# Seven block products in place of eight in the down projection of an MLP (Trainium2, one core)

## The chip, the cores and the metric

The kernel runs as one program on one core of a Trainium2 chip. The metric is the device time of one execution in microseconds (us). Three runs of the kernel before gave 1694.85, 1695.14 and 1696.07 us, with a median of 1695.14.

## The reference

One block of an encoder over 1024 tokens of width 1024, in float32. Two branches (latent attention with 8 heads, and a bidirectional mLSTM with 4 heads) are merged by gates, and an MLP follows. The part that matters here is the end:

```
x = x + merged @ w_out
u = rmsnorm(x, norm_mlp_g) @ w_mlp_up          # (1024 x 1024) @ (1024 x 4096)
x = x + square(relu(u)) @ w_mlp_down           # (1024 x 4096) @ (4096 x 1024)
return rmsnorm(x, norm_final_g)
```

## The kernel before, in words

TensorE multiplies in the format fp32r. To keep float32 accuracy each operand is split in two: `h` is a cast to fp32r on ScalarE (line 79), and `l` is the rest, source minus `h`, by a subtraction on VectorE (line 80). A product of two blocks is then three matmuls, h by h, h by l and l by h; l by l is left out. So each operand that TensorE reads costs one instruction on ScalarE and one on VectorE, and each 128x128x512 block product costs three matmuls.

The program runs in stages. First come the input projections and the mLSTM cores (to about 390 us). Within and after them the gates are made: `gate_a` for 8 column blocks, spread among the heads, and `gate_b` for 8 more (390 to 510 us); their results go to DRAM for later. Attention follows (to 850 us), then the merge and the output projection (to 1005 us), the up projection (1036 to 1327 us) and the down projection (1327 to 1685 us).

The up projection already works with seven block products in place of eight, the Winograd form of Strassen's scheme. The 4096 hidden channels are taken as 16 pairs of 128-channel blocks (`up_pair(p)`, lines 1160 to 1187). For each pair seven products of 12 matmuls run. Their right operands, sums and differences of blocks of x ("T1" to "T4" and plain blocks), were made once and stay in SBUF. Their left operands ("S1" to "S4") are sums of weight blocks and are made on VectorE by `Pair.sums` (lines 1108 to 1123). For the first five pairs two of the seven products are done ahead of the loop. `activate` applies relu and square on ScalarE and writes the hidden block to DRAM.

The down projection is a plain product (lines 1282 to 1350). The 32 blocks of 128 hidden channels are taken in 8 groups of four (FC = 4). For each block `down_in` loads the hidden block [128, 1024] and the weight rows [128, 1024] from DRAM, and splits both. Then, for each of 8 token tiles, 24 matmuls (4 blocks, 2 halves of the columns, 3 products) run into two PSUM banks, and `finish` adds the two banks, scaled by the token's norm factor `rsq`, to the residual `xm` of that token tile (line 1321, VectorE). `xm` stays in SBUF for the whole stage (8 tiles). In the last group `finish` also makes the final norm (lines 1324 to 1329) and writes the output.

Nearly all SBUF tiles come from one pool of 46 slots of 4 KB per partition (`slot`, NSLOT = 46). Raw data that is to be split comes into a second pool of 4 buffers of the same size (`wp`, NWR = 4). PSUM has two tiles of two banks (`bankA`) and four of one (`bankB`). All loads and stores in question are issued by SyncE (SP), in order. A planner of the framework fixes the order of the instructions on each engine when the program is built: instructions have the order of the program text as their priority, and one that is not ready, or has no free slot, lets later ones pass. `tc.high_priority` moves instructions forward in this order; `finish` used it. On the chip each engine then executes its list in order.

Of the kernel before, what the change touches and what calls it, by code (L numbers as in the profile page):

```python
# [18 lines left out]
P = 128  # L19
# [19 lines left out]
def kernel(ctx: ExitStack, tc: tile.TileContext, x, positions, norm_mix_g, w_in, mla_q_norm_g,  # L39
# [748 lines left out]

    def gate_a(ms):
        for m in ms:  # L790
# [8 lines left out]
            siga.append(dt_)  # L799

    def gate_b():
        for m in range(8):
# [15 lines left out]
            dump("brb", s, lambda o, m=m: o[m])  # L818

# [268 lines left out]
    class Pair:  # L1088
# [19 lines left out]
        def sums(self):  # L1108
            a, b = self.raw
            u, v = slot([P, 2, 4, P], F32, "ws"), slot([P, 2, 4, P], F32, "ws")  # L1110
            nc.vector.tensor_tensor(out=u[:, 0], in0=b[:, 0:4], in1=b[:, 4:8], op=ALU.add)
            nc.vector.tensor_tensor(out=u[:, 1], in0=u[:, 0], in1=a[:, 0:4], op=ALU.subtract)
            h, l = slot([P, 2, 4, P], F32R, "wh"), slot([P, 2, 4, P], F32R, "wl")
            split(h, l, u)
            self.ops["S1"], self.ops["S2"] = [(h[:, i], l[:, i]) for i in range(2)]
            nc.vector.tensor_tensor(out=v[:, 0], in0=a[:, 0:4], in1=b[:, 0:4], op=ALU.subtract)
            nc.vector.tensor_tensor(out=v[:, 1], in0=a[:, 4:8], in1=u[:, 1], op=ALU.subtract)
            h, l = slot([P, 2, 4, P], F32R, "wh"), slot([P, 2, 4, P], F32R, "wl")
            split(h, l, v)
            self.ops["S3"], self.ops["S4"] = [(h[:, i], l[:, i]) for i in range(2)]  # L1120
            w = slot([P, 2, 4, P], F32R, "w22")
            split(w[:, 0], w[:, 1], b[:, 4:8])
# [6 lines left out]
    hidd = [dr.tile([P, 1024], F32, tag="hid", name=nm("hid"), bufs=DFF // P) for _ in range(DFF // P)]  # L1129
# [24 lines left out]
    def activate(p, j, r):  # L1154
# [3 lines left out]
        nc.sync.dma_start(out=hidd[2 * p + j], in_=r.rearrange("p a n -> p (a n)"))  # L1158

    def up_pair(p):  # L1160
        add = lambda o, x_, y_: nc.vector.tensor_tensor(out=o, in0=x_, in1=y_, op=ALU.add)
        r0, b1 = early.pop(p, None), None
# [7 lines left out]
        r1 = slot([P, 2, 512], F32, "r")  # L1170
# [10 lines left out]
        add(r1[:, 1], b3, u[:, 1])  # L1181
        product(b2, p, "22", "T4", False)
        add(r1[:, 0], b2, m1)
        activate(p, 1, r1)
        product(b3, p, "S4", "22", False)
        add(r0[:, 1], b3, u[:, 0])
        activate(p, 0, r0)
# [63 lines left out]
    pairs[0].sums()  # L1251
    for q in range(2):
# [18 lines left out]

    for p in range(NP):
        if p + 1 < NP:
            pairs[p + 1].load()
            if p + 1 >= EARLY:
                pairs[p + 1].plain()
            pairs[p + 1].sums()
# [97 lines left out]
```

## Time and profile before

| what | value |
|---|---|
| median of 3 runs | 1695.14 us |
| the profiled execution | 1694.64 us |
| its span, first to last instruction | 1692.9 us |
| TensorE matmul (PE) busy | 1651.5 us, 8613 matmuls |
| VectorE (DVE) busy | 927.9 us |
| ScalarE (ACT) busy | 684.2 us |
| GpSimd (POOL) busy | 188.5 us |
| moved by DMA | 139.68 MB |
| granted clock of TensorE, mean | 0.994 |

How to read it: the profile is of one execution; the 1.74 us between its time and its span lie before the first and after the last instruction. Matmuls overlap each other in the pipeline, so the sum of their durations is larger than the time that they take; the number of matmuls in a stretch tells the rate. "Idle before" is the time that an engine stood still just before an instruction, with what ended it.

### The profile page before, as it was taken

The numbers are of one execution on the slowest core, as the hardware profiler recorded it, in microseconds if no ns is written. First come the engines' busy times: TensorE is split into PE (matmuls) and PEld (weight loads), VectorE is DVE, ScalarE is ACT, GpSimd is POOL, SyncE is SP. The second block draws the span as 40 slices with busy tenths as digits, with TensorE's granted clock in tenths as the row PEclk, the third lists the DMA queues.
The fourth block names the chain that finished last, engine by engine and source line by source line (L and its number), as shares of the span: only waits on it lengthen the run. The fifth ranks groups of instructions, "written<-read, shape, count | busy, mean of one in ns | idle before, by whom it ended". The sixth has DMA issues, their size and how long they took to land. (4 is left out here: it accounts for less than half of the span.)

```text
span 1692.9 us, 21982 instructions
## 1 busy us (share of the span) xinstructions
PE 1651.5 (98%) x8613; PEld 1391.0 (82%) x8613; DVE 927.9 (55%) x1405; ACT 684.2 (40%) x1211; POOL 188.5 (11%) x363
## 2 busy tenths in 40 slices
PE   7999999999999999999999997999999999999998
PEld 6789989888879979889888875778888788888886
DVE  5776756633223287787876236654554564444424
ACT  6254444432122376666743325554444421111101
POOL 4112020100001433333300000000000000000001
PEclk9999999999999999999999998999999999999999
DMA  7111110112212000000057312543333752332002
GB/s 215 38 38 55 46 38 13 57 63 67 89 62 94 1 13 1 2 13 1 8 195 246 112 50 75 149 132 118 100 100 113 276 195 100 100 100 100 25 1 100
DMA packets 112651, 139.68 MB, mean 83 GB/s; under 512 B 5971, under 2 KB 88868, under 8 KB 112548
## 3 DMA queue, kind: packets, MB, share of 16 engines
q1 hardware_dynamic: 112516, 138.28, 25.1%
q8 instruction: 68, 1.11, 0.3%
q14 instruction: 35, 0.29, 0.1%
q10 hardware_dynamic: 32, 0.01, 0.0%
HBM read 104.71 MB, written 33.55 MB: 82 GB/s over the span
## 5 line engine op out<-in xcount | busy, mean ns | idle before, releaser
L1311 PE MATMUL b<-wh,hh 128*128 128x512 f32 x512 | 201.1, 394 | 1.1 <-DVE xm L1321 1.1
L227 PE MATMUL a<-th,wh 128*128 128x512 f32 x504 | 202.1, 401 | 0.0
L228 PE MATMUL a<-tl,wh 128*128 128x512 f32 x504 | 201.7, 400 | 0.0
L1312 PE MATMUL b<-wl,hh 128*128 128x512 f32 x512 | 201.2, 394 | 0.0
L79 ACT CAST wh<-wr 128x1024 fp32r<-128x1024 f32 (+6 forms) x118 | 111.0, 962 | 193.4 <-PE b L1312 162.6
L1321 DVE SCALAR_TENSOR_TENSOR xm<-b,rsq,xm 128x512 f32<-128x512 f32 x128 | 90.1, 746 | 157.4 <-PE b L1315 157.1
L232 PE MATMUL a<-th,wl 128*128 128x512 f32 x504 | 162.9, 400 | 0.0
L204 PE MATMUL a<-wh,th 128*128 128x256 f32 (+5 forms) x504 | 161.9, 322 | 0.2 <-ACT mo L569 0.2
L1139 PE MATMUL b<-bh,wh 128*128 128x512 f32 x384 | 152.1, 398 | 9.2 <-ACT wh L79 9.2
L205 PE MATMUL a<-wl,th 128*128 128x256 f32 (+5 forms) x504 | 160.4, 319 | 0.3 <-DVE wl L80 0.3
L206 PE MATMUL a<-wh,tl 128*128 128x256 f32 (+5 forms) x504 | 160.4, 319 | 0.0
L1315 PE MATMUL b<-wh,hl 128*128 128x512 f32 x512 | 160.1, 393 | 0.0
L1139 PE MATMUL b<-bl,wh 128*128 128x512 f32 x384 | 151.7, 395 | 0.0
L1139 PE MATMUL b<-bh,wl 128*128 128x512 f32 x384 | 150.7, 395 | 0.1
L80 DVE TENSOR_TENSOR wl<-wr,wh 128x1024 fp32r<-128x1024 f32 (+6 forms) x118 | 131.3, 1128 | 23.5 <-ACT wh L79 19.0
L306 POOL TENSOR_SCALAR m<-m 128x1 f32<-128x1 f32 (+1 forms) x40 | 9.0, 225 | 1172.7 <-ACT o L1326 830.5
L1311 PEld LDWEIGHTS b<-wh,hh 128*128 128x128 f32 x512 | 96.1, 188 | 23.7 <-DVE xm L1321 1.5
L1315 PEld LDWEIGHTS b<-wh,hl 128*128 128x128 f32 x512 | 96.1, 188 | 22.8
L1312 PEld LDWEIGHTS b<-wl,hh 128*128 128x128 f32 x512 | 96.2, 188 | 22.3
L227 PEld LDWEIGHTS a<-th,wh 128*128 128x128 f32 x504 | 94.7, 188 | 21.1 <-issue 1.0
L228 PEld LDWEIGHTS a<-tl,wh 128*128 128x128 f32 x504 | 94.7, 188 | 20.7 <-issue 0.5
L232 PEld LDWEIGHTS a<-th,wl 128*128 128x128 f32 x504 | 94.0, 188 | 21.2 <-issue 0.2
(287 smaller groups left out, 3309.8 us busy)
## 6 DMA issues: line engine op xcount, KB each, us to landing
wr<-in_w_mlp_up SPq DMA_DIRECT2D x37, 512.0 KB
hid<-r SPq DMA_DIRECT2D x32, 512.0 KB, 2.6
u<-hid SPq DMA_DIRECT2D x32, 512.0 KB, 4.5
wr<-in_w_mlp_down SPq DMA_DIRECT2D x32, 512.0 KB
wr<-in_w_in SPq DMA_DIRECT2D x24, 512.0 KB, 3.8
x<-in_x SPq DMA_DIRECT2D x8, 512.0 KB, 5.7
da<-sg SPq DMA_DIRECT2D x8, 512.0 KB, 2.6
db<-sg SPq DMA_DIRECT2D x8, 512.0 KB, 2.6
```

The source lines that it names most:

```text
L79: nc.scalar.copy(out=h, in_=src)
L80: (eng or nc.vector).tensor_tensor(out=l, in0=src, in1=h.bitcast(F32), op=ALU.subtract)
L204: nc.tensor.matmul(out=ps, lhsT=xh, rhs=wh, start=(k == 0), stop=False)
L205: nc.tensor.matmul(out=ps, lhsT=xh, rhs=wl, start=False, stop=False)
L206: nc.tensor.matmul(out=ps, lhsT=xl, rhs=wh, start=False, stop=(k == n - 1))
L227: nc.tensor.matmul(out=o, lhsT=wts[k][0], rhs=xh, start=(k == 0), stop=False)
L228: nc.tensor.matmul(out=o, lhsT=wts[k][0], rhs=xl, start=False, stop=False)
L232: nc.tensor.matmul(out=o, lhsT=wts[k][1], rhs=xh, start=False, stop=(k == n - 1))
L1139: nc.tensor.matmul(out=o, lhsT=x_[:, k], rhs=y_, start=(first and k == 0 and i == 0), stop=(k == 3 and i == 2), skip_group_check=True)
L1311: nc.tensor.matmul(out=pos[n], lhsT=a[:, ts_], rhs=wh[:, c], start=(i == 0), stop=False)
L1312: nc.tensor.matmul(out=pos[n], lhsT=a[:, ts_], rhs=wl[:, c], start=False, stop=False)
L1315: nc.tensor.matmul(out=pos[n], lhsT=b[:, ts_], rhs=wh[:, c], start=False, stop=(i == FC - 1))
```

## The change

The down projection is done in the Winograd form too. The hidden matrix is cut in two along the tokens and in two along the channels (the even and the odd block of a pair), and w_mlp_down in two along the channels and in two along its columns. Of the seven left operands three are plain blocks of the hidden matrix and four are sums or differences of blocks, and so for w_mlp_down on the right. The sums are not made in the down stage:

- The weight sums are made in the gate stages. After each of the 8 steps of `gate_a` and of `gate_b` one call of `down_sums` loads a pair of weight blocks, makes four differences on VectorE, and writes them to DRAM.
- The hidden sums are made at the end of `up_pair` by `keep`: four operations on VectorE, and seven writes of [128, 512] to DRAM in place of two of [128, 1024].
- Within `up_pair` the preparation of the next pair, which stood ahead of the call, is spread among the products, `sums` is cut in three (`sums`, `plain_22`, `sums_14`), and the raw weights are loaded a pair earlier.
- The down projection takes the 16 pairs in 4 groups of four (GD = 4). In a group, phases 0, 1 and 2 have two products each and phase 3 has one; a product covers four token tiles with 12 matmuls each. The seven partial results are added in five pairs of accumulators in SBUF ("m1", "11", "12", "22", "21"; 10 slots), and only in the last group do they come to `xm`, which is loaded at its start.

```diff
+    def down_sums(p):
+        y, z = slot([P, 2, 512], F32, "wy"), slot([P, 2, 512], F32, "wz")
...
+        nc.sync.dma_start(out=y, in_=rows[:, :, 0:512])
+        nc.sync.dma_start(out=z, in_=rows[:, :, 512:1024])
+        a, b = slot([P, 2, 512], F32, "wt"), slot([P, 2, 512], F32, "wt")
+        nc.vector.tensor_tensor(out=b[:, 1], in0=z[:, 0], in1=y[:, 0], op=ALU.subtract)
+        nc.vector.tensor_tensor(out=a[:, 0], in0=z[:, 1], in1=b[:, 1], op=ALU.subtract)
+        nc.vector.tensor_tensor(out=a[:, 1], in0=z[:, 1], in1=z[:, 0], op=ALU.subtract)
+        nc.vector.tensor_tensor(out=b[:, 0], in0=y[:, 1], in1=a[:, 0], op=ALU.subtract)
+        nc.sync.dma_start(out=wd_d[p][:, 0:2, :], in_=a)
+        nc.sync.dma_start(out=wd_d[p][:, 2:4, :], in_=b)
...
@@ gate_a, gate_b
+            down_sums(summed.pop(0))
...
+    def keep(p, r0, r1, u):
+        f = slot([P, 512], F32, "hs")
+        nc.vector.tensor_tensor(out=u[:, 1], in0=r0[:, 1], in1=r1[:, 1], op=ALU.add)
+        nc.vector.tensor_tensor(out=u[:, 0], in0=u[:, 1], in1=r0[:, 0], op=ALU.subtract)
+        nc.vector.tensor_tensor(out=r0[:, 1], in0=r0[:, 0], in1=r0[:, 1], op=ALU.subtract)
+        nc.vector.tensor_tensor(out=f, in0=r1[:, 0], in1=u[:, 0], op=ALU.subtract)
+        for j, src in ((0, r0[:, 0]), (1, r1[:, 0]), (2, u[:, 0]), (3, r0[:, 1]), (4, r1[:, 1]), (5, u[:, 1]), (6, f)):
+            nc.sync.dma_start(out=hid_d[p][:, j, :], in_=src)
...
     def up_pair(p):
+        nx = pairs[p + 1] if p + 1 < NP else None
+        if p + 2 < NP:
+            pairs[p + 2].load()
...
+        if nx and p + 1 >= EARLY:
+            nx.plain()
         product(b2, p, "S3", "T3", False)
         add(u[:, 1], b2, m1)
+        if nx:
+            nx.sums()
+        r1 = slot([P, 2, 512], F32, "r")
...
+        activate(r0)
+        keep(p, r0, r1, u)
...
+    GD = 4
+    def raw_pair(srcs):
+        r = wp.tile([P, 2, 512], F32, tag="wr", name=nm("wr"))
+        for j, src in enumerate(srcs):
+            nc.sync.dma_start(out=r[:, j], in_=src)
+        return r
+    def in_pair(srcs):
+        r = raw_pair(srcs)
+        h, l = slot([P, 2, 512], F32R, "dh"), slot([P, 2, 512], F32R, "dl")
+        split(h, l, r)
+        return [(h[:, j], l[:, j]) for j in range(2)]
...
+    def operands(p, ph):
+        if ph == 3:
+            return in_last(p)
+        right = ([down_row(p, 0)[:, 0:512], down_row(p, 1)[:, 0:512]] if ph == 0 else
+                 [wd_d[p][:, 2 * (ph - 1) + j, :] for j in range(2)])
+        return [in_pair([hid_d[p][:, 2 * ph + j, :] for j in range(2)]), in_pair(right)]
+    def take(name, pr, j, bank, fresh=False):
...
+        if fresh:
+            nc.scalar.copy(out=o, in_=bank)
+        else:
+            nc.vector.tensor_tensor(out=o, in0=bank, in1=o, op=ALU.add)
+    def dmul(o, tt, ops, j, first, order):
+        c = slice(tt * P, (tt + 1) * P)
+        for n, i in enumerate(order):
+            (ah, al), (bh, bl) = ops[i][0][j], ops[i][1][j]
...
+            nc.tensor.matmul(out=o, lhsT=ah[:, c], rhs=bh, start=st, stop=False, skip_group_check=True)
+            nc.tensor.matmul(out=o, lhsT=ah[:, c], rhs=bl, start=False, stop=False, skip_group_check=True)
+            nc.tensor.matmul(out=o, lhsT=al[:, c], rhs=bh, start=False, stop=en, skip_group_check=True)
...
+    def settle_in(name, tt, part):
+        t = tt + 4 * part[0]
+        o = acc[name, tt // 2][:, tt % 2]
+        if name != "11":
+            nc.vector.tensor_tensor(out=o, in0=o, in1=acc["m1", tt // 2][:, tt % 2], op=ALU.add)
+        c = slice(part[1] * 512, (part[1] + 1) * 512)
+        nc.vector.scalar_tensor_tensor(out=xm[t][:, c], in0=o, scalar=rsq[:, t:t + 1], in1=xm[t][:, c], ...)
+    def final(tt, part, bank):
...
+        nc.vector.scalar_tensor_tensor(out=xm[t][:, c], in0=bank, scalar=rsq[:, t:t + 1], in1=xm[t][:, c], ...)
...
+    nxt = [operands(p, 0) for p in range(GD)]
+    for g in range(NG):                     # NG = 4 groups
...
+            for tt in range(4):             # phase 0, first product (first group: operand by operand)
+                dmul(h_(tt), tt, ops, 0, True, every)
+        for pr in range(2):
+            take("m1", pr, None, b3(A[pr]), first_group)
+        nxt = [operands(p, 1) for p in group]
+        for tt in range(4):                 # second product, added in the same banks
+            dmul(h_(tt), tt, ops, 1, False, every)
...
+        nxt = [operands(p, 2) for p in group]          # between the two products of phase 1
...
+        ops, ops3 = nxt, [operands(p, 3) for p in group]
...
+        else:                               # last group, phases 2 and 3
+            for tt in range(4):
+                for name, part in (("22", (1, 1)), ("21", (1, 0)), ("12", (0, 1))):
+                    settle_in(name, tt, part)
+            for tt in range(4):
+                dmul(h_(tt), tt, ops, 1, True, every)
+                final(tt, (1, 1), h_(tt))
+                dmul(Bk[tt], tt, ops, 0, False, every)
+                final(tt, (1, 0), Bk[tt])
+                finish(tt + 4)
+                dmul(h_(tt), tt, ops3, 0, False, every)
+                final(tt, (0, 1), h_(tt))
+                finish(tt)
```

## Rows read from the trace of the kernel before

**Rows 1.** Head of the page: span, then busy time, share and instructions.

```profile
span 1692.9 us, 21982 instructions
PE 1651.5 (98%) x8613; PEld 1391.0 (82%) x8613; DVE 927.9 (55%) x1405; ACT 684.2 (40%) x1211; POOL 188.5 (11%) x363
```

**Rows 2.** What TensorE waited for, whole span: us in total, times, longest.

```profile
PE b L1139 <- ACT wh L79: 9.2, 2, 8.8
...
PE b L1311 <- DVE xm L1321: 1.1, 1, 1.1
```

**Rows 3.** Stretches of the span: busy time of each engine, granted clock, DMA.

```profile
core 0: us, PE busy (x) PEld busy (x) DVE busy (x) ACT busy (x) POOL busy (x), PEclk, DMA share, GB/s
1047.00:1117.00 70.00, 69.16 (x294) 54.45 (x295) 45.16 (x61) 30.75 (x33) 0.00 (x0) 1.00 0.46 136
1117.00:1325.00 208.00, 208.00 (x898) 167.73 (x897) 101.33 (x134) 93.04 (x109) 0.00 (x0) 1.00 0.33 107
1350.00:1440.00 90.00, 90.00 (x391) 73.04 (x390) 49.20 (x56) 22.02 (x22) 0.00 (x0) 1.00 0.47 159
1327.00:1685.00 358.00, 356.57 (x1539) 288.47 (x1537) 169.22 (x196) 72.31 (x77) 5.20 (x14) 1.00 0.32 112
80.00:400.00 320.00, 319.08 (x1911) 276.56 (x1910) 202.22 (x353) 144.64 (x333) 40.66 (x74) 1.00 0.16 46
390.00:512.00 122.00, 120.31 (x518) 97.53 (x517) 32.45 (x45) 20.55 (x25) 0.52 (x16) 0.99 0.26 83
```

**Rows 4.** Groups by line, the matmuls of the down stage: busy us, mean ns | idle before.

```profile
L1311 PE MATMUL b<-wh,hh 128*128 128x512 f32 x512 | 201.1, 394 | 1.1 <-DVE xm L1321 1.1
...
L1312 PE MATMUL b<-wl,hh 128*128 128x512 f32 x512 | 201.2, 394 | 0.0
...
L1315 PE MATMUL b<-wh,hl 128*128 128x512 f32 x512 | 160.1, 393 | 0.0
```

**Rows 5.** Groups by line and shape from 1170 us on, VectorE and ScalarE.

```profile
L1321 DVE SCALAR_TENSOR_TENSOR xm<-b,rsq,xm 128x512 f32<-128x512 f32 x128 | 90.1, 746 | 157.4 <-PE b L1315 157.1 <-DMA xm<-xmd 0.3
...
L80 DVE TENSOR_TENSOR wl<-wr,wh 128x1024 fp32r<-128x1024 f32 x38 | 46.4, 1221 | 8.3 <-ACT wh L79 8.2
L79 ACT CAST wh<-wr 128x1024 fp32r<-128x1024 f32 x38 | 39.9, 1051 | 186.6 <-PE b L1312 162.6 <-DMA wr<-in_w_mlp_down 17.9 <-DVE xm L1321 6.1
...
L1328 DVE SCALAR_TENSOR_TENSOR o<-xm,m,gf 128x1024 f32<-128x1024 f32 x8 | 10.3, 1284 | 17.8 <-POOL m L308 17.8
...
L1161 DVE TENSOR_TENSOR r<-b,r 128x512 f32<-128x512 f32 x8 | 5.5, 691 | 4.3 <-PE b L1139 4.3
...
L1112 DVE TENSOR_TENSOR ws<-ws,wr 128x512 f32<-128x512 f32 x7 | 4.8, 682 | 0.0
```

**Rows 6.** The end of the span in order of time: start us, us.

```profile
1684.03 0.62 PE L1315 MATMUL b<-wh,hl 128*128 128x512 f32 x2
1684.46 1.41 DVE L1321 SCALAR_TENSOR_TENSOR xm<-b,rsq,xm 128x512 f32<-128x512 f32 x2 [0.66 <-PE b L1315]
1685.96 1.06 ACT L1326 ACTIVATE o<-xm 128x1024 f32<-128x1024 f32 x1 [4.39 <-DVE xm L1321]
...
1688.06 1.28 DVE L1328 SCALAR_TENSOR_TENSOR o<-xm,m,gf 128x1024 f32<-128x1024 f32 x1 [2.19 <-POOL m L308]
```

**Rows 7.** What ScalarE waited for from 1340 us on.

```profile
ACT wh L79 <- PE b L1312: 162.6, 6, 32.1
...
ACT hh L79 <- DMA u<-hid: 18.8, 17, 2.8
```

**Rows 8.** What TensorE waited for from 80 to 400 us.

```profile
PE b L761 <- issue: 0.6, 1, 0.6
...
```

**Rows 9.** What ScalarE waited for from 80 to 400 us.

```profile
...
ACT raw L593 <- DVE acc L588: 20.7, 7, 7.3
...
```

**Rows 10.** DMA issues: count, KB each, median us to landing.

```profile
u<-hid SPq DMA_DIRECT2D x32, 512.0 KB, 4.5
```

**Rows 11.** Line 798 alone: durations ns min/median/max, first and last start.

```profile
L798 SPq DMA_DIRECT2D da<-sg x8: 338/338/343, 86.6 to 369.4; - x8
```

More of the change, by code (lines that the diff above doesn't have):

```diff
@@ L1128 @@
     B = {}
-    hidd = [dr.tile([P, 1024], F32, tag="hid", name=nm("hid"), bufs=DFF // P) for _ in range(DFF // P)]
+    hid_d = [dr.tile([P, 7, 512], F32, tag="hid", name=nm("hid"), bufs=NP) for _ in range(NP)]
     xmd = [dr.tile([P, 1024], F32, tag="xmd", name=nm("xmd"), bufs=8) for _ in range(8)]
@@ L1251 @@
     pairs[0].sums()
+    pairs[0].plain_22()
+    pairs[0].sums_14()
     for q in range(2):
@@ L1269 @@
     nc.vector.reciprocal(out=rsq, in_=rsq)
+    pairs[1].load()
     for p in range(NP):
[L1273 to L1277, printed above, removed]
[L1278 to L1295 removed]
@@ L1297 @@
-    nxt = [down_in(f) for f in range(FC)]
-    for f0 in range(0, NF, FC):
-        hid, wd = [n[0] for n in nxt], [n[1] for n in nxt]
-        last = f0 + FC == NF
+        up_pair(p)
+    GD = 4
[9 more added lines that the diff above has]
+        return [(h[:, j], l[:, j]) for j in range(2)]
@@ new lines, in final @@
+    def final(tt, part, bank):
+        t = tt + 4 * part[0]
+        c = slice(part[1] * 512, (part[1] + 1) * 512)
+        nc.vector.scalar_tensor_tensor(out=xm[t][:, c], in0=bank, scalar=rsq[:, t:t + 1], in1=xm[t][:, c],
+                                       op0=ALU.mult, op1=ALU.add)
+    NG = NP // GD
+    nxt = [operands(p, 0) for p in range(GD)]
+    xm = [None] * 8
+    every = range(GD)
+    for g in range(NG):
+        first_group, last = g == 0, g == NG - 1
+        group = range(g * GD, (g + 1) * GD)
@@ L1331 @@
-        nxt = []
-        for t2 in range(4):
-            pair = [(t, [bankB(), bankB()]) for t in (2 * t2, 2 * t2 + 1)]
-            if f0 == 0:
-                for t, _ in pair:
-                    xm[t] = slot([P, 1024], F32, "xm")
-                    nc.sync.dma_start(out=xm[t], in_=xmd[t])
-            if f0 == 0 and t2 == 0:
-                for i in range(FC):
-                    for t, pos in pair:
-                        down(t, i, pos)
-                for t, pos in pair:
-                    finish(t, pos)
-            else:
-                for t, pos in pair:
-                    for i in range(FC):
-                        down(t, i, pos)
-                    finish(t, pos)
-            if not last:
-                nxt.append(down_in(f0 + FC + t2))
+        ops = nxt
@@ new lines @@
+        nxt = [operands(p, 1) for p in group]
+        for tt in range(4):
+            dmul(h_(tt), tt, ops, 1, False, every)
+        for pr in range(2):
+            if last:
+                for j in range(2):
+                    settle_in("11", 2 * pr + j, (0, 0))
+                    final(2 * pr + j, (0, 0), h_(2 * pr + j))
+            else:
+                take("11", pr, None, b3(A[pr]), first_group)
+        ops = nxt
+        Bk = [bankB() for _ in range(4)]
+        for tt in range(4):
+            dmul(Bk[tt], tt, ops, 0, True, every)
+            take("12", tt // 2, tt % 2, Bk[tt], first_group)
```

120 lines of the change are left out of this document (72 added, 48 removed).

## Prediction

> **What bounds the kernel now.** I read the head of the page first: TensorE's matmuls are busy for 98% of the span, VectorE for 55%, ScalarE for 40% [rows 1]. Since matmuls overlap, the share alone proves little, so the waits of TensorE come next: the largest is one of 8.8 us ahead of the up projection, and the only one of the down stage is 1.1 us at its start [rows 2]. Then the stretches: in the down stage, 1327 to 1685 us, 1539 matmuls fill 358 us while VectorE is busy for 169 and ScalarE for 72 [rows 3]. The kernel is bound by the number of matmuls that TensorE issues, nearly everywhere. So a change gains what it takes from that number, as long as the new operands arrive in time, and work on other engines is free as long as it stays beside matmuls. The groups by line show the down stage as three lines of 512 matmuls each, 1536 in all [rows 4].
>
> **The price of a matmul.** The mean of 394 ns in its row [rows 4] is a duration with overlap. The rate is read from a stretch without a wait: 390 issues (391 records, one shared with the border) in the 90 us from 1350 on make 0.2308 us each [rows 3]. In the up stage, whose products are issued in the order h-h, h-l, l-h that the new down stage uses, 898 matmuls in 208 us make 0.2316. So the new order costs nothing per matmul, and I take 0.2308.
> The Trainium skill ("TensorE: Matmul & The Clock Gate", section "Wait — 56ns, not 53.3ns?") gives 215.7 ns from start to start for 512 columns at full clock. By it the same count would give back 41.4 us, an estimate from that page; the row is 7% slower at a granted clock of 1.00, so the row decides.
>
> **What is removed.** A group of the new stage has three phases of two products and one of a single product, seven; a product is four token tiles by 12 matmuls, 48. Seven by 48 by four groups is 1344 matmuls in place of 1536. Gone: 192 x 0.2308 = 44.3 us. The new stage then needs 1344 x 0.2308 = 310.2 us of TensorE.
>
> **What is added, stage by stage.**
>
> *Gate stages.* 16 calls of `down_sums`, each four operations of 128x512 from SBUF to SBUF. The nearest row is the weight sum of line 1112, 682 ns [rows 5]: 2.73 us a call, 43.6 us in all, half before 390 us and half after. From 80 to 400 us VectorE is busy for 202 of 320 us, from 390 to 512 for 32 of 122 [rows 3]; with the sums that is 224 of 320 and 54 of 122. Each call also has four DMAs on SP at about 0.34 us [rows 11], 1.4 us of SP's queue; the weight loads of the next step stand behind them. The cover is TensorE's lead: its largest wait in the first stretch was 0.6 us [rows 8]. What speaks for a cost are the slots: ScalarE already waits 20.7 us there at line 593 for a `raw` tile that VectorE still reads [rows 9], and each call holds four more slots for a load (4.5 us for 512 KB by the nearest load [rows 10]), its operations, and a store. Bounds: -1 us (the little that TensorE waits could fall away with a new order) to 22 us (each of the first eight calls delays a core's chain by its 2.73 us, uncovered); the later eight stand beside an engine that idles for half of the time. I take 1.5, near the row of 0.6.
>
> *Up stage.* `keep` adds four operations per pair, 2.73 us, on VectorE; seven stores in place of two add 5 x 0.34 = 1.7 us on SP. From 1047 to 1117 us, five pairs, VectorE goes from 45 to 59 of 70 us; from 1117 to 1325, eleven pairs, from 101 to 131 of 208 [rows 3]. It stays under TensorE in both, tightest in the first (84%). Queued behind `keep` on VectorE are the additions that free a PSUM bank for the next product; a bank that comes back 2.7 us late is covered by another product, 12 x 0.2308 = 2.8 us, in another bank. The raw weights come a pair (84 x 0.2308 = 19.4 us) earlier, ahead of those stores on SP, so the stores delay nothing that is due. The cut of `sums` moves work and adds none. Bounds: -0.5 (the waits there are about that) to 5 x 2.7 = 14 us; I take 0.5.
>
> *Start of the down stage.* The operands of phase 0 need 16 slots. The last pair has no successor to prepare, and each of its products frees four slots of a right operand, so they come while it runs. The first product goes operand by operand: 12 matmuls, 2.8 us, against two splits, 2 x 1.221 = 2.4 us on VectorE [rows 5]. Before, the same passage cost 1.1 us [rows 2]. I take no difference; the bounds are -1 and the four pairs of splits uncovered, 9.8 us.
>
> *Groups 1 to 3 of the down stage.* A group has 8 + 8 + 8 + 4 = 28 splits where there were 16 per 8 blocks: 112 in place of 64 (1.221 us on VectorE, 1.051 on ScalarE [rows 5]). VectorE has 28 x 1.221 = 34.2 us of splits and 28 x 0.69 = 19.3 us of adding banks to the accumulators (the 691 ns of line 1161 [rows 5], in the first group mostly on ScalarE), 53.5 us per group against 336 x 0.2308 = 77.5 us of TensorE. Loads are 28 x 512 KB per group, 189 GB/s by this sum, against 159 GB/s at a DMA share of 0.47 now [rows 3]; SP issues 56 halves, 19 us of 77.5. The four raw buffers allow 4 x 2.77 = 11.1 us from load to release, and a load takes 4.5 [rows 10] plus 2.3 for both splits. Slots: 10 accumulators, 16 for the running phase, 16 for the next: 42 of 46. The next phase can be prepared while the present one runs, so nothing is exposed. I take 0.5 us for all three; the upper end stands with the rivals.
>
> *Last group.* Two things change. `xm` and the final gain hold 9 more slots: 10 + 9 + 16 + 16 = 51 of 46, so the last three splits of phase 1, and of phase 2, start only when the phase before ends, operand by operand. The first operands are there, so TensorE is held for about one split on either engine, 1.05 + 1.22 us at most at each of two handovers less what the first operands cover; I take 1.5 each, 3 us, between 0 and the eight splits of a phase in full, 9.8 each. And VectorE must do 20 splits (24.4), the bank additions (4 x 0.69 + 8 x 0.69 = 8.3), four products straight to `xm` from the accumulator and four from the bank (8 x 0.746 = 6.0), twelve settlements (12 x (0.682 + 0.746) = 17.1), twelve last additions (9.0) and eight final products of 1.284 us (10.3): 75.1 us beside 77.5. It just fits if the settlements of "21" and "12" are moved forward into its gaps, and a backlog at the end is likely.
>
> *Tail.* After the last matmul two operations of line 1321 (1.41 us) become one, so -0.7 us; then ScalarE, GpSimd, VectorE and the store as before [rows 6]. `finish` of the other half's tile stands in the same queue and no longer has the priority that it had. With the backlog I take +1 us net, between -0.7 and 6.
>
> **Sum.** The profiled execution took 1694.64 us: 1692.9 of span [rows 1] and 1.74 around it. -44.3 + 1.5 + 0.5 + 0 + 0.5 + 3 + 1 = -37.8 gives 1656.8; the median of the runs is 0.5 us above that execution. I say 1656.
>
> **Rivals.**
>
> *The slots serialise the down stage* (slower). If the next phase's operands get no slots until the present one is done, each of the 15 handovers shows its eight splits, 8 x 1.221 = 9.8 us, 146 us in all, and the time is 1694.6 - 44.3 + 146 = 1796. It decides from 44.3 / 9.8 = 4.5 such handovers on. For it: in the old down stage ScalarE waits 162.6 us for slots that TensorE still reads [rows 7]. Against it: those waits reach 32 us and TensorE does not follow, and 42 of 46 fit by my count; it needs tiles released later than their last reader. With the last group's two handovers in full it is 1656.8 - 3 + 19.6 = 1673.
> Beside it the Trainium skill ("Perfetto Trace Analysis", section "Optimization Strategy") says that the same gap repeating on the engine that should be saturated can mean too little SBUF or PSUM for the next tile. No such gap is in this trace before; after, gaps of TensorE at the end of each phase would be this sign.
>
> *The gate stages pay for the sums.* Eight calls beside the mLSTM cores at 2.73 us, or their slots, hold the cores' chains: up to 22 us, so 1657 to 1677. For it the wait of line 593, against it 0.6 us of TensorE waiting.
>
> *The gain is nearly whole.* The planner fills all gaps: 1694.6 - 44.3 - 0.7 = 1649.6.
>
> *VectorE sets the pace in the last group.* The 75.1 us meet waits, a tenth of it is lost and the tail shows it: 8 to 10 us more than I take, 1665.
>
> That the products aren't fewer is excluded by the count.
>
> **Chances and range.** Forecast, 1652 to 1662: 0.45. Nearly whole: 0.15. Last group: 0.16. Gate stages: 0.13. Slots: 0.11, of which 0.07 ends slower. A run differs from another by some 0.1%, so 0.2% (3.4 us) is what a measurement can tell from no change. Faster 0.90; same 0.03, where slots or gate stages eat just the 44 us; slower 0.07. The range is 1648 to 1680: from just under the whole gain to just over the last group's two handovers in full, or the gate stages' upper end (1677).
>
> **What would show it.** Three groups of matmuls of 448 each at 0.231 us apart; a down stage of about 315 us; VectorE at 74% in it (112 splits 137, banks and `xm` about 92 of 310 us). TensorE's waits up to 1327 us as before within 3 us. In the last group, waits of 1 to 2 us for ScalarE's or VectorE's splits at two handovers, and VectorE without a gap in its last 33 us. It is wrong if TensorE waits regularly in the first three groups (slots, or four raw buffers too few for the loads), if waits appear before 512 us, or if the up stage's 19.4 us per pair grow.

## The result: 18.4 us gained, where 39 were forecast

The changed kernel takes 1676.56 us (median of four runs, 1676.23 to 1677.49), the kernel before took 1694.99 (also four runs); the ratio is 0.9892, with a 95% interval of 0.9875 to 0.9909. It is faster by 1.1%, and the time lies in the range (1648 to 1680), but the gain is less than half of the forecast. So 44 us of matmuls went, and some 26 us came back.

### The profile after

The head of the page, to be held against [rows 1]:

```profile
span 1675.1 us, 22459 instructions
PE 1614.1 (96%) x8421; PEld 1358.4 (81%) x8421; DVE 1051.5 (63%) x1551; ACT 745.0 (44%) x1275; POOL 196.0 (12%) x363
```

8613 - 8421 = 192 matmuls fewer: the change does what it says. TensorE's share falls from 98 to 96%, which is the first sign that it now waits. What it waits for (us in total, times, longest), against [rows 2]:

```profile
PE b L204 <- ACT wh L79: 7.6, 1, 7.6
PE b L1167 <- ACT wh L79: 7.1, 1, 7.1
...
PE a L1376 <- ACT dh L79: 4.8, 1, 4.8
PE b L1167 <- DVE u L1198: 4.7, 5, 1.1
...
PE a L1377 <- DVE dl L80: 2.7, 2, 2.0
...
PE a L1376 <- DVE xm L1401: 1.4, 1, 1.4
PE b L689 <- DVE cst L693: 1.2, 1, 1.2
```

The second row is the wait of 8.8 us ahead of the up projection [rows 2], a little shorter. The others are new or have grown: one at L204, which is the start of the latent stage (1.0 us before); five at L1167 for a `u` in the up stage (one of 0.8 us before); two kinds at the start of the down stage (`dh`, `dl`); one of 1.4 us in its last group (`xm`); and one of 1.2 us that ends at 254.8 us, in a core of the mLSTM (`cst`). The stretches of the span, with the columns of [rows 3]:

```profile
core 0: us, PE busy (x) PEld busy (x) DVE busy (x) ACT busy (x) POOL busy (x), PEclk, DMA share, GB/s
503.00:519.00 16.00, 8.42 (x34) 6.69 (x33) 10.07 (x23) 5.52 (x7) 0.00 (x0) 0.79 0.34 134
1047.00:1117.00 70.00, 65.36 (x273) 50.12 (x271) 47.74 (x70) 34.59 (x40) 0.00 (x0) 1.00 0.47 158
1117.00:1325.00 208.00, 207.63 (x896) 168.34 (x897) 136.07 (x186) 95.05 (x108) 0.00 (x0) 1.00 0.44 151
1325.00:1404.00 79.00, 70.64 (x289) 54.77 (x288) 39.46 (x39) 40.79 (x46) 0.00 (x0) 0.96 0.62 206
1404.00:1640.00 236.00, 236.00 (x1022) 191.50 (x1021) 167.10 (x173) 87.60 (x89) 0.00 (x0) 1.00 0.61 204
1640.00:1667.00 27.00, 24.56 (x103) 18.53 (x101) 15.11 (x17) 8.05 (x14) 5.98 (x14) 1.00 0.29 117
```

Read the first two columns together. From 1404 to 1640 us TensorE is full (236.00 of 236), at 236 / 1022 = 0.231 us per matmul: the body of the new down stage runs exactly as it was priced. So does the up stage from 1117 us on. What is not full are the passages between: 8.42 of 16 us around 511 us, 65.36 of 70 in the first up pairs, 70.64 of 79 at the start of the down stage.

To put a size on each passage, compare the start of the n-th matmul in both traces (n counted from the first; up to the down stage both kernels have the same matmuls, within an up pair partly in another order, and no record is missing). How much later it comes in the changed kernel:

| passage | shift at its end | what it adds | forecast |
|---|---|---|---|
| to 26 us, the first matmuls | +1.1 | +1.1 | none |
| to 503 us, gate stages (nearly all at 253 us, where the wait for `cst` stands) | +2.5 | +1.4 | 1.5, both rows together |
| 503 to 519 us, start of the latent stage | +9.2 | +6.7 | |
| 519 to 1036 us | +7.4 | -1.8 | none |
| 1036 to 1340 us, up stage (all of it before 1137) | +12.5 | +5.1 | 0.5 |
| first matmul of the down stage | +17.5 | +5.0 | 0 |
| to 1404 us, its first group | +23.7 | +6.3 | 0 |
| the rest of the down stage | | +2.0 | 3.5 |
| tail | | +0.7 | 1 |

In sum 26.5; 44.3 less 26.5 is the 17.8 by which the span is shorter (1692.9 to 1675.1). The first line is not the change's: in the profiles of the variants below, whose first microseconds are the same program, it lies between -0.4 and +1.1.

### Three passages, line by line

**At 510 us.** VectorE, ScalarE and TensorE, in order of time (start us, us; in brackets the idle time before and what ended it):

```profile
509.44 1.23 DVE L836 TENSOR_TENSOR sg<-a,sg 128x1024 f32<-128x1024 f32 x1 [2.96 <-PE a L232]
510.58 0.68 DVE L802 TENSOR_TENSOR wt<-wz,wt 128x512 f32<-128x512 f32 x1
...
512.38 0.48 DVE L407 TENSOR_TENSOR s<-posT,s 128x128 f32<-128x128 f32 x2
...
515.47 0.29 DVE L419 TENSOR_SCALAR s<-s 128x256 f32<-128x256 f32 x1
515.79 0.42 ACT L420 ACTIVATE rot<-s 128x256 f32<-128x256 f32 x1 [9.56 <-DVE s L419]
516.12 1.55 ACT L79 CAST wh<-wr 128x768 fp32r<-128x768 f32 x2
...
516.98 1.01 PE L204 MATMUL b<-wh,th 128*128 128x384 f32 x2 [7.58 <-ACT wh L79]
```

The page puts the 7.6 us down to the cast of a weight, but ScalarE had idled for 9.56 us ahead of it: its queue is in order, and the sine of the rotary tables (L420) stands before the casts. The sine waits for the tables (L407 to L419), and these stand on VectorE behind the last call of `down_sums`, which stands behind the last gate's multiplication, which waits for TensorE. In the kernel before, L412 to L419 ran from 503.0 to 505.3, ahead of that multiplication (there L814):

```profile
503.02 0.29 DVE L412 TENSOR_SCALAR s<-s 128x256 f32<-128x256 f32 x1
...
504.98 0.29 DVE L419 TENSOR_SCALAR s<-s 128x256 f32<-128x256 f32 x1
506.92 1.23 DVE L814 TENSOR_TENSOR sg<-a,sg 128x1024 f32<-128x1024 f32 x1 [1.65 <-PE a L232]
```

**At 1069 us.**

```profile
1066.50 0.69 DVE L1190 TENSOR_TENSOR u<-r,r 128x512 f32<-128x512 f32 x1 [2.22 <-ACT r L1185]
...
1068.43 0.68 DVE L1193 TENSOR_TENSOR hs<-r,u 128x512 f32<-128x512 f32 x1
...
1069.03 0.68 DVE L1198 TENSOR_TENSOR u<-b,r 128x512 f32<-128x512 f32 x1
...
1069.77 0.50 PE L1167 MATMUL b<-bh,wh 128*128 128x512 f32 x1 [1.13 <-DVE u L1198]
```

`keep` (L1190 to L1193) waits for ScalarE's squares, and VectorE idles for 2.22 us in front of it, with the addition that frees TensorE's bank queued behind. The same four lines come again at 1084, 1100 and 1116 us: four gaps of 1.5 us between matmuls.

**At 1340 us.**

```profile
1341.91 1.06 ACT L1185 ACTIVATE r<-r 128x1024 f32<-128x1024 f32 x1
1342.87 3.87 ACT L79 CAST dh<-wr 128x1024 fp32r<-128x1024 f32 x4
...
1343.00 0.69 DVE L1190 TENSOR_TENSOR u<-r,r 128x512 f32<-128x512 f32 x1 [2.21 <-ACT r L1185]
...
1345.54 4.62 DVE L80 TENSOR_TENSOR dl<-wr,dh 128x1024 fp32r<-128x1024 f32 x4
...
1344.90 1.09 PE L1376 MATMUL a<-dh,dh 128*128 128x512 f32 x2 [4.84 <-ACT dh L79]
1347.94 0.80 PE L1377 MATMUL a<-dl,dh 128*128 128x512 f32 x1 [1.96 <-DVE dl L80]
```

Not one operand of the down stage is cast before the last pair's squares are done at 1342.9, though two raw tiles had been loaded since 1300 us. Then the two splits come one after the other, with TensorE standing still.

### The profile page after: what moved, and what is told of

The parts are those of the page before. It is cut to its first block, busy times and chain, and to the rows that moved or that the text cites. A ratio compares the mean times of both kernels' runs of the same rounds, so it can differ in the third digit from the quotient of the medians.

```text
span 1675.1 us, 22459 instructions
## 1 busy us (share of the span) xinstructions
PE 1614.1 (96%) x8421; PEld 1358.4 (81%) x8421; DVE 1051.5 (63%) x1551; ACT 745.0 (44%) x1275; POOL 196.0 (12%) x363
## 4 chain that ended last, share of the span: by engine, by line
PE 86%; DVE 5%; ACT 3%; issue 3%; POOL 1%; DMA 1%; SPq 0%; POOLq 0%; ACTq 0%; DVEq 0%
PE b L1167 17%; PE a L232 7%; PE a L228 7%; PE a L227 7%; PE a L204 5%; PE a L205 5%; PE a L206 5%; PE b L1007 3%; PE a L1377 3%; PE a L1378 3%; PE a L1376 3%; PE b L1377 2%; PE b L1376 2%; PE b L1378 2%; PE a L986 2%
## 5 line engine op out<-in xcount | busy, mean ns | idle before, releaser
L79 ACT CAST dh<-wr 128x1024 fp32r<-128x1024 f32 x112 | 114.2, 1049 | 157.3 <-PE a L1377 49.0
L80 DVE TENSOR_TENSOR dl<-wr,dh 128x1024 fp32r<-128x1024 f32 x112 | 134.1, 1221 | 62.0 <-ACT dh L79 61.3
L1167 PE MATMUL b<-bh,wh 128*128 128x512 f32 x384 | 151.2, 399 | 11.6 <-ACT wh L79 7.1
L204 PE MATMUL a<-wh,th 128*128 128x256 f32 (+5 forms) x504 | 161.6, 321 | 0.2 <-ACT mo L569 0.2
L1167 PE MATMUL b<-bl,wh 128*128 128x512 f32 x384 | 152.2, 396 | 0.0
L1167 PE MATMUL b<-bh,wl 128*128 128x512 f32 x384 | 150.7, 396 | 0.0
L1377 PE MATMUL a<-dl,dh 128*128 128x512 f32 x256 | 101.9, 398 | 2.7 <-DVE dl L80 2.7
L80 DVE TENSOR_TENSOR wl<-wr,wh 128x1024 fp32r<-128x1024 f32 (+6 forms) x86 | 93.2, 1096 | 15.8 <-ACT wh L79 11.8
L1378 PE MATMUL a<-dh,dl 128*128 128x512 f32 x256 | 101.5, 397 | 0.0
L204 PEld LDWEIGHTS a<-wh,th 128*128 128x128 f32 x504 | 95.2, 189 | 6.7 <-ACT P L993 0.5
L205 PEld LDWEIGHTS a<-wl,th 128*128 128x128 f32 x504 | 95.2, 189 | 6.4 <-DVE wl L80 0.8
L206 PEld LDWEIGHTS a<-wh,tl 128*128 128x128 f32 x504 | 95.1, 189 | 5.4
L1167 PEld LDWEIGHTS b<-bh,wh 128*128 128x128 f32 x384 | 72.7, 189 | 31.8 <-ACT wh L79 8.5
```

Of the source, the lines that this page charges most:

```text
L79: nc.scalar.copy(out=h, in_=src)
L80: (eng or nc.vector).tensor_tensor(out=l, in0=src, in1=h.bitcast(F32), op=ALU.subtract)
L204: nc.tensor.matmul(out=ps, lhsT=xh, rhs=wh, start=(k == 0), stop=False)
L205: nc.tensor.matmul(out=ps, lhsT=xh, rhs=wl, start=False, stop=False)
L206: nc.tensor.matmul(out=ps, lhsT=xl, rhs=wh, start=False, stop=(k == n - 1))
L1167: nc.tensor.matmul(out=o, lhsT=x_[:, k], rhs=y_, start=(first and k == 0 and i == 0), stop=(k == 3 and i == 2), skip_group_check=True)
```

## The experiments

Each edit is made on the changed kernel unless said otherwise. The kernel before took 1694.1, 1695.0 and 1694.3 us on the three occasions; ratios are to that.

**1. The last call of the sums one step away.** Two calls at one earlier step of the second gate, none at the last:

```
-            down_sums(summed.pop(0))
+            for _ in range((1, 1, 1, 2, 1, 1, 1, 0)[m]):
+                down_sums(summed.pop(0))
```

> The changed kernel, but gate_b makes no weight sums after its last step; step 3 makes two pairs instead. Theory A: TensorE's wait of 8.0 us at the first latent product (at 509 us) comes from the last call of down_sums: its four operations stand on VectorE ahead of the rotary tables, the sine of these stands on ScalarE ahead of the casts of the latent weights. Then the wait falls back to about 1.4 us as in the kernel before, and the time goes from 1676.6 to about 1670 (-6.7, the step of the ledger between 503 and 520 us). Rival B: a general load of VectorE and of SP in the gate stage delays the weights; one call more at step 3 makes up for it and the time stays within 2 us.

Measured: 1671.98 us, ratio 0.9872 (0.9857 to 0.9886). The step between 503 and 519 us falls from 6.7 to 0.2: the tables now run from 505.85 to 508.10 us, ahead of the gate's multiplication (L836, 509.68). Of the 6.7 us that were expected some 4 are left (3.7 by the medians against the kernel before, 4.6 without it), since 1.2 us come up at the step with two calls and 1.3 us more in the down stage.

The row of 503 to 519, to be held against the same stretch above:

```profile
503.00:519.00 16.00, 14.04 (x62) 12.45 (x61) 9.54 (x17) 7.82 (x10) 0.00 (x0) 0.89 0.41 134
```

62 matmuls where there were 34; 28 x 0.231 are the 6.5 us by which the step fell.

**2. The tables first.** All sixteen calls stay where they are; the tables and the sine are emitted ahead of the second gate:

```
-    weave((gate_b(), 1.0))
     rotary()
+    weave((gate_b(), 1.0))
```

> The changed kernel with all 16 calls of down_sums in their places, but the rotary tables made ahead of gate_b. Theory A: the sine no longer stands behind the last sums, so the casts of the latent weights run early and the wait of 8.0 us is gone or nearly so: about 1670. Rival C: the sums on VectorE and their four DMAs delay the latent weights directly (loads queued on SP, rest halves queued on VectorE): the wait stays at 4 us or more and the time within 3 us of 1676.6.

Measured: 1674.51 us, ratio 0.9885 (0.987 to 0.99). The 7.6 us wait is gone, one of 3.3 us for a `wl` stands in its place, and the step falls from 6.7 to 1.8; about 2 us come up where the tables now stand. So the time falls by only 1 to 2 us, where 6.6 were expected, and the step is what tells: it is the order of sums and tables, from either side, and not the sums' work: 1.8 us of additions cannot hold TensorE for 6.7, but the 3.4 us of tables and the sine behind them can.

**3. The sums alone.** The kernel before, with the sixteen calls added and their results read by nothing:

```
             siga.append(dt_)
+            down_sums(summed.pop(0))
...
             dump("brb", s, lambda o, m=m: o[m])
+            down_sums(summed.pop(0))
```

> The kernel before with one addition: the sixteen calls of down_sums in the gate stages, whose results nothing reads; the up and down stages are those of before. It prices the sums alone. Theory A (the last call stands ahead of the rotary tables on VectorE, so that the latent stage starts late): the step of about 6.7 us between 504 and 519 us is there, with the 1.5 us at 253 us, and nothing else: 1694 + 8 = 1702 us (1700 to 1703.5). Rival (the steps in the gate stages come from what the new up and down stages do to the order of the whole program): 1694 to 1697.

Measured: 1702.23 us, ratio 1.0044 (1.0027 to 1.006), 7.3 us by the medians. The shift against the kernel before rises by 1.5 at 253 us and by 6.7 between 503 and 519, and does not grow after; the wait is the same to the tenth:

```profile
PE b L204 <- ACT wh L79: 7.6, 1, 7.6
```

So the gate stages' 8 us are the sums' alone, and neither the new up stage nor the down stage has a part in them.

**4. The last pair's seventh sum without a tile of its own.** `f` is written over `r1[:, 0]` once that has been stored, for the last pair alone:

```
-        f = slot([P, 512], F32, "hs")
+        f = r1[:, 0] if p == NP - 1 else slot([P, 512], F32, "hs")
```

> The changed kernel, but for the last pair the seventh hidden sum is written over a block that is already stored, so that it takes no slot of its own. Theory A (slots in order of the text): the tile of this sum is the last one ahead of the operands of the down stage, and it is given its slot only after the last activation, so all casts of the down stage wait for that. Without it the first four casts run beside the last pair's matmuls: TensorE's waits of 5.2 and 2.6 us at 1340 to 1348 us and the stretch at half clock behind them go, 8 to 11 us, about 1667. Rival B: four raw buffers; the operands of pairs 2 and 3 come late whatever the slots do: the first wait goes, 5 us, but waits behind it stay, about 1672. Rival C: ScalarE and VectorE are too busy at the end of the last pair: within 2 us of 1676.6.

Measured: 1666.89 us, ratio 0.9848 (0.983 to 0.9865). From the last up matmul to 1404 us the shift grows by 2.0 instead of 11.3. ScalarE in the passage:

```profile
1327.67 3.89 ACT L79 CAST dh<-wr 128x1024 fp32r<-128x1024 f32 x4
1336.09 1.06 ACT L1184 ACTIVATE r<-r 128x1024 f32<-128x1024 f32 x1 [4.53 <-DVE r L1203]
```

Four casts now run ahead of the last pair's squares, where in the changed kernel they came behind them. One tile of 128x512 had held up everything: tiles come out of one pool in the order of the program's text, `keep` of the last pair stands in it ahead of the down stage's operands, and its `hs` had to wait for a tile to come free. That an instruction without a free slot lets later ones pass, as the description of the planner says, did not help here: the four casts stand behind `hs` in the text, and they came 15 us later with it than without it.

**5. The last pair's `keep` behind the operands.** The other way round: `hs` stays, the whole `keep` is emitted later.

```
     nxt = [operands(p, 0) for p in range(GD)]
+    keep(*late.pop())
```

> The changed kernel with the last up pair's keep (its four VectorE operations, the tile of its seventh sum and its seven stores) emitted behind the operands of the down stage's first 64-matmul block, in place of ahead of them; everything it computes is unchanged, and its seventh sum keeps a tile of its own. Theory A (tiles are handed out in the order of the text: the seventh sum's tile waits for the last pair's neighbours and blocks the down stage's first casts): the 5.2 us wait at 1339.7 and the 2.6 us behind it go, as in the run that gave the sum no tile of its own: -9 us, 1667 to 1669. Rival (the stores of the last pair or its four VectorE operations hold up the down stage, not the tile): moving them behind the casts on VectorE helps too, but the loads of the last pair are late and no gain over -5 is left, 1671 to 1675.

Measured: 1666.47 us, ratio 0.9836 (0.9822 to 0.9849), the same as in 4 within its interval. The four casts stand at 1327.97, and TensorE's longest wait in the passage is 2.2 us; the shift grows by 3.7 there. Experiment 4 takes away the tile (and stores one block earlier), with `keep`'s four operations where they were; this one moves the tile and all the rest. Both bring the casts forward by the same 15 us, so the tile's place in the text is shown as the cause, and the rival's price for the late stores (no gain over 5) is not there.

**6. The order of products in the first five pairs.** S1 was emitted ahead of S3, to give VectorE more time for the addition.

```
+        if p < EARLY:
+            product(b3, p, "S1", "T1", True)
         product(b2, p, "S3", "T3", False)
```

> The changed kernel, but for the first five pairs the product S1 stands ahead of S3 in the text, so that it lies between S2 and S3, which share a bank. Theory A: TensorE's four waits of 1.5 us from 1068 to 1117 us arise because S3 follows S2 at once and has to wait until VectorE has read the bank; with S1 in between they go: -5.4, about 1671. Rival B: keep's 2.7 us on VectorE is the cause, and a bank comes back late whichever product stands there: less than 2 us gained.

Measured: 1677.14 us, ratio 0.9902 (0.9887 to 0.9916): no gain. The theory behind it fell: in pairs two to five, where the gaps lie, the operands of TensorE's matmuls follow each other in the same order by name in both traces, and S1's result is added without a wait for TensorE (1074.60 us in the changed kernel). So the order had already been S2, S1, S3: the planner had drawn S1 forward. Only the first pair, which has no gap, was reordered. TensorE waits for `u` in the same places, 5.6 us in all. It also says that the 12 matmuls of S1 do stand between, 2.8 us, and are too few.

**7. `keep` of the first five pairs one addition later.** It is emitted in the next pair, behind the first addition:

```
         add(u[:, 0], b2, m1)
+        if late:
+            keep(*late.pop())
...
-        keep(p, r0, r1, u)
+        if p < EARLY:
+            late.append((p, r0, r1, u))
+        else:
+            keep(p, r0, r1, u)
```

> The changed kernel with one move: for the first five up pairs the four VectorE operations and seven stores of keep are emitted one pair later, behind the next pair's first add (u[:, 0] = S2's bank + m1), so that this add stands ahead of them on VectorE. In the changed kernel's timeline the add runs at 1069.03, behind keep's four (1066.50 to 1069.03), which wait for ScalarE's squares, and TensorE's S3 product waits for it until 1069.77. Theory B (keep stands in front of the add that S3's bank waits for): the four waits of about 1.5 us at 1068, 1084, 1100 and 1116 go, the step of 5.4 us in the first five pairs falls to about 1, and the time falls by 4 to 5.5 us, to 1671 to 1672.5. Rival (the products' own order is the cause: fewer products of the next pair stand between those of one bank, whoever is first on VectorE): the waits stay, 1676 to 1677.

Measured: 1668.07 us, ratio 0.9844 (0.9829 to 0.9859), 3 us below what theory B said. TensorE waits for no `u` in the up stage any more. VectorE in the passage:

```profile
1064.08 0.69 DVE L1200 TENSOR_TENSOR u<-b,r 128x512 f32<-128x512 f32 x1 [1.61 <-PE b L1167]
1064.69 0.69 DVE L1190 TENSOR_TENSOR u<-r,r 128x512 f32<-128x512 f32 x1
...
1066.63 0.68 DVE L1193 TENSOR_TENSOR hs<-r,u 128x512 f32<-128x512 f32 x1
```

The addition comes as soon as TensorE has the bank ready, and `keep` fills the time in which VectorE had idled. The up stage's part of the shift goes from +5.1 to -2.0, so it is now 2 us shorter than in the kernel before; the other 1.2 us are the first matmuls, which differ from run to run. The Trainium skill ("Perfetto Trace Analysis", section "Optimization Strategy") reads a gap that repeats as a possible lack of SBUF or PSUM for the next tile. Here a gap repeated four times and went with no buffer added, so the queue's order was the cause.

**8. `keep` of the first five pairs on GpSimd.**

```
+        eng = nc.gpsimd if p < EARLY else nc.vector
-        nc.vector.tensor_tensor(out=u[:, 1], in0=r0[:, 1], in1=r1[:, 1], op=ALU.add)
+        eng.tensor_tensor(out=u[:, 1], in0=r0[:, 1], in1=r1[:, 1], op=ALU.add)
...
```

> The changed kernel with keep's four operations of the first five up pairs on GpSimd instead of VectorE, their place in the text unchanged. Theory B (keep occupies VectorE ahead of the add): the four waits of about 1.5 us go and the time falls by 4 to 5.5 us, to 1671 to 1672.5, as when keep is emitted later. Rival (the products' own order): the waits stay, 1676 to 1677. A third way: GpSimd's operations take about twice as long as VectorE's 0.69 us and hold the tiles longer, so that a later pair waits for a slot: the four waits go and others come, 1673 to 1677.

Measured: 1676.27 us, ratio 0.989 (0.9875 to 0.9905): no gain. The waits shrink, but others take their place, and the rows show another way than the one expected (tiles held longer). GpSimd's first two operations, and VectorE beside them:

```profile
1065.74 1.73 POOL L1191 TENSOR_TENSOR u<-r,r 128x512 f32<-128x512 f32 x1 [206.10 <-DVE u L1199]
1067.55 1.63 POOL L1192 TENSOR_TENSOR u<-u,r 128x512 f32<-128x512 f32 x1
```

```profile
1065.64 0.68 DVE L1135 TENSOR_TENSOR ws<-wr 128x512 f32<-128x512 f32 x1
1066.24 1.78 DVE L1137 TENSOR_TENSOR ws<-wr,wr 128x512 f32<-128x512 f32 x1
1067.94 1.78 DVE L1136 TENSOR_TENSOR ws<-ws,wr 128x512 f32<-128x512 f32 x1
...
1071.35 0.68 DVE L1199 TENSOR_TENSOR u<-b,r 128x512 f32<-128x512 f32 x1
```

The sums of the next pair's weights, 0.69 us each alone, take 1.78 and stretch the preparation that was meant to be relieved.

**9. The edits together.** Experiment 1 (here with the two calls at the gate's first step), 4 and 7:

> The changed kernel with three edits together: the last gate step's call of down_sums made at the second gate's first step instead (two calls there, none at the last), keep of the first five pairs emitted behind the next pair's first add, and the last pair's seventh sum written over a stored tile in place of a slot of its own. If the three losses are separate, their parts add: 1676.6 - 5.5 to 6.5 (latent start) - 4 to 5.5 (first pairs) - 9.3 (start of the down stage) = 1655.5 to 1658 us. If one loss takes the place of another (a wait that is only moved to the next product), 1660 to 1667.

Measured: 1656.92 us, ratio 0.9779 (0.9764 to 0.9793). The three losses are nearly separate: alone the edits gained 3.7, 8.8 and 8.5 us over the change, 21.0 in all, and together 19.6 (each by the medians against the kernel before of its occasion). At the last matmul of the up stage the shift against the kernel before is -0.3 where it was +12.5. The same kernel once more:

> The kernel with the three edits (two calls of the sums at the second gate's first step and none at its last, keep of the first five pairs behind the next pair's first add, the last pair's seventh sum without a tile of its own), as measured at 1656.9, in more rounds: 1656 to 1658.

Measured: 1656.55 us, ratio 0.9778 (0.9765 to 0.9791). In this profile the step with two calls cost 3.7 us, in the first one 1.4, of the same program. TensorE's wait there (for a `wl`, at 405 us) is 1.9 us against 1.1, and behind it the granted clock is 0.50 from 406.8 to 410.2 us, the level of 1.2 GHz, where in the first profile it stays at 1.00. Why the wait is longer is open, and it bounds what one profile can tell of a passage of this kind.

**10. The last pair's `keep` late as well.** As 9, with the edit of 5 in place of 4, so that neither the tile nor VectorE's four operations stand ahead of the operands.

> The three edits with another third one: the last pair's keep is emitted behind the down stage's first operands, so that it neither takes a tile nor VectorE ahead of them (with the seventh sum written over a stored tile, four VectorE operations of keep still stood from 1332.08 to 1334.88 ahead of the last split of the first block, and TensorE waited 1.1 us for it). If that wait is all: 1656.9 - 1.5 = 1655.4. If the last pair's stores, now later, hold up loads of the first group: 1657 to 1660.

Measured: 1655.31 us, ratio 0.9774 (0.9761 to 0.9787). The wait of 1.0 us for `dl` in the second profile of 9 is gone, that for `dh` (1.2 there, 1.3 here) has stayed; the difference of 1.2 us to 9 is within the intervals.

**11. The last group's priority restored.** As 10, with the bodies of `finish` and `final` put under `tc.high_priority(offset=HPM)`, as the kernel before had its `finish`.

> As the kernel with the late keep, and the eight finish and sixteen final of the last group put ahead of other ready work, as the kernel before had them (high_priority with the same offset). The wait of 1.75 us for xm at 1635.7 behind the output's scaling, and the 0.8 us of the tail, should shrink if their order on VectorE is their cause: 1 to 2 us less than the kernel without it. If the bank is simply handed over at once whatever the order, no difference (within 1 us).

Measured: 1654.68 us, ratio 0.9771 (0.9757 to 0.9785), 0.6 us less than 10, which is no difference that this measurement can tell. What TensorE waited for in it:

```profile
PE b L205 <- DVE wl L80: 2.0, 1, 2.0
...
PE a L1384 <- DVE xm L1411: 1.6, 3, 0.7
PE b L1384 <- ACT dh L79: 1.4, 1, 1.4
PE a L232 <- DVE wl L80: 1.3, 1, 1.3
```

The longest wait for `xm` went from 1.4 to 0.7 us, and small ones came. This is the fastest version that was run: 39.7 us below the kernel before, of the 44.3 that the matmuls are worth.

## Why the prediction was wrong

**What held.** The count and the price: 192 fewer at 0.231 us. The body of the down stage: groups without a wait from 1404 to 1640 us, so the slots did not serialise it (that rival asked for 4.5 handovers of 9.8 us). The splits came out as forecast in number and length:

```profile
L80 DVE TENSOR_TENSOR dl<-wr,dh 128x1024 fp32r<-128x1024 f32 x112 | 134.1, 1221 | 62.0 <-ACT dh L79 61.3
```

Tail: 1 forecast, 0.7 measured, with `finish` of the other tile ahead of the last `xm` on VectorE, as described.

**What came near by luck.** The last group and the groups before it: 3.5 forecast, 2.0 measured, but not by the handovers that were named. TensorE waits for no split in the last group. Its one wait there is for a bank:

```profile
1656.89 1.28 DVE L1385 SCALAR_TENSOR_TENSOR o<-xm,m,gf 128x1024 f32<-128x1024 f32 x1 [0.72 <-POOL m L308]
1658.09 0.74 DVE L1401 SCALAR_TENSOR_TENSOR xm<-a,rsq,xm 128x512 f32<-128x512 f32 x1
...
1658.89 0.50 PE L1376 MATMUL a<-dh,dh 128*128 128x512 f32 x1 [1.39 <-DVE xm L1401]
```

VectorE reads that bank (L1401) only behind the output's scaling (L1385), which itself waited for GpSimd. Nor was VectorE without a gap at the end: from 1636 to 1669 us it was busy for 20.1 of 33 us, and in the whole down stage for 67% of the time (215 of 322 us), where 74% was forecast.

**What failed.** Three terms failed, by 6.6, 4.6 and 11.3 us, 22.5 together; the lines without a term, the last group and the tail give 2.5 of it back.

**Gate stages, "I take 1.5, near the row of 0.6".** Measured 8, inside the stated bounds (-1 to 22), and with the sign that the prediction had named, waits before 512 us. The place was wrong as well as the size. I priced the first eight calls by the cores' chain and called the later eight safe, since "the later eight stand beside an engine that idles for half of the time". An idle engine is no cover for work that stands in front of something due: the 6.7 us are all the last call's, by what is queued behind it. The rival "the gate stages pay for the sums" gave the time that was found, 1657 to 1677, but by the wrong mechanism: of the 26.5 us only the 1.4 before 503 us can be the cores'. What puts the tables behind the sums is not settled: the tables' tiles come behind the sums' tiles in the text, and the planner may also have ranked them so. Moving either took the 7.6 us wait away, which does not tell the two apart. The 1.4 us at 253 us are the wait for `cst`, which also comes with the sums alone (experiment 3); what delays it was not tried.

**Up stage, "a bank that comes back 2.7 us late is covered by another product, 12 x 0.2308 = 2.8 us".** Measured 5.1, inside the bounds of -0.5 to 14. The step counted `keep`'s four operations as the lateness, and left out that they wait themselves: VectorE idled for 2.2 us for ScalarE's squares with the addition ready behind. The bank of S2 was ready at about 1065.7 us and its addition ran at 1069.03, 3.3 late, and with the addition's own 0.7 that is 4.0 against a cover of 2.8. I named what is queued behind the new work, not what the new work waits for. It ended after the first five pairs, where VectorE is tightest, as the step said; the other eleven cost nothing. But these five are also the pairs with two products made ahead of the loop, so that fewer products stand between S2 and S3, and no run tells the two reasons apart.

**Start of the down stage, "so they come while it runs ... I take no difference".** Measured 5.0 and 6.3, just beyond the upper bound of 9.8. With one tile out of the way (experiment 4), or with the same tile later in the text (experiment 5), the operands do come while the last pair runs, so the count of tiles was not the fault; their order was. I counted how many are needed, not who stands before them in the text. `keep` adds one tile per pair, 16 in all, and the last one stands ahead of the very first operand. Part of the second number is the clock: behind the wait the granted clock was at half, from 1345 to 1352 us, the level of 1.2 GHz, and the matmuls stood 0.43 us apart there. In experiment 4, where TensorE's waits in the passage were 1.5 and 0.5 us, it was 1.00 from 1325 to 1392.

**The sum as a whole.** With the three orders mended the time is 1654.7 to 1656.9, where 1656 was forecast. The matmuls were priced rightly; what failed is that the new work would be placed well by itself. That the mended sum meets the forecast so closely is in part luck: the mended up stage gives 2.0 us back (experiment 7), which no term had.

## What to carry on

Work that is moved beside an idle engine is priced in two numbers, not in one: its duration, and what stands behind it in that queue, with the wait that it brings of its own. An operation that waits for a third engine is emitted behind what is ready first: experiment 7 left the four operations on VectorE, moved them behind one addition, and all waits for `u` were gone. Where all tiles come from one pool, a new small tile at the end of a stage is checked against the first operands of the next.

## What the runs showed of the hardware

**VectorE and GpSimd slow each other.** In experiment 8 an addition of two tiles in SBUF took VectorE 1.78 us while GpSimd worked, and 0.69 without it; the first one, which had begun 0.1 us ahead of GpSimd's, took 0.68. An addition that reads a PSUM bank and one tile took 0.68 (1071.35) with GpSimd's fourth operation running from 1070.84. GpSimd is slowed too: its first two additions took 1.73 and 1.63 us, and 1.32 at 1128.32, where VectorE stood idle. The Trainium skill ("SBUF — State Buffer", section "Who interferes with whom") says that a VectorE instruction with two SBUF inputs contends with a GpSimd instruction that reads SBUF, through a pair of ports that the two share, and that the order of issue decides which one waits. The rows agree: the slowed addition that began at 1066.24 ended at 1068.02, 0.55 us after GpSimd's first (1067.47), the next one 0.54 us after GpSimd's second (1069.18). I had expected GpSimd to be slow, not to pass its slowness on.

**How long the clock stays at half differs between executions.** Before the change the granted clock of the latent stage's start was 0.50, the level of 1.2 GHz, from 510.1 to 513.5 us, behind a wait of 0.95 us. After it, with a wait of 7.6 us, it was 0.50 from 512.2, within the wait, to 522.5, but in the profile of experiment 5, with the same 7.6 us, only from 513.3 to 520.2. In the first profile of experiment 9, where the wait is 2.0 us, no such stretch is there, and one of 3.4 us comes at 608 us; in the second one, with the same wait, it was 0.50 from 516.0 to 519.4. So the length of the wait alone does not set it.
